# Decoder step with four linear-recurrent mixers: block transposes in the delta-rule inverse, plain copies at score levels 32 and 64, selections over all rows

## The chip, the core and the metric

One core of a Trainium2 chip runs the kernel: TensorE (PE, with its weight loads shown as PEld), VectorE (DVE), ScalarE (ACT), GpSimd (POOL) and SyncE (SP, which issues the DMAs here) work side by side from queues of their own and meet at semaphores. The metric is the time of one execution on the device in microseconds; lower is better.

## What is computed

Two trunk layers over 256 prompt tokens and 8 x 4 sample tokens (288 columns in all), width 1024, f32. Each layer is a half-step SwiGLU network, the token mixing, and a second half-step SwiGLU network, each closed by a layer norm with shift, scale and gate from a conditioning vector. The token mixing has four mixers of four heads: retention, GLA, HGRN2 and gated DeltaNet. Three of them are gated recurrences:

```python
S_t = diag(exp(g_t)) S_{t-1} + k_t v_t^T,  o_t = S_t^T q_t      # _gla_scan
att = einsum('bhtd,bhsd,bhtsd->bhts', qc, kc, decay); o = att @ vc + (qc * exp(G)) @ S
```

The fourth, gated DeltaNet, solves a unit lower triangular system per chunk:

```python
a = where(strict, bc * (kc @ kc.T) * L, 0.0)
tm = eye + a
u = triangular_solve(tm, bc * vc); w = triangular_solve(tm, bc * exp(G) * kc)
delta = u - w @ S
```

## The kernel before

All work is recorded first as operations and then put in order by a scheduler in the file itself (class `Rec`, `schedule`): each operation has a cost and a priority (the longest path behind it), and `LB` adds a shift to the priority by the name of the section (`inv0` is the inverse of layer 0) and the engine. `STAY` lets PE stay with one shape of matmul, `PEN` weighs a change of ScalarE's function table, `HOLD` lets an engine wait for a better operation. Almost every operation therefore has the helper's line, L547, in the profile, and is found by its tiles.

The large products (feed-forward, the input projections of the mixing `win`, its output projection `wout`) are made of three matmuls each: ScalarE rounds a weight tile to `whi`, VectorE subtracts it to `wlo`, and PE multiplies `whi` with the high and low halves of the input (`hh`, `hl`) and `wlo` with `hh`. Weights come by DMAs of 512 KB on SP's queue into three buffers `st`. The conditioning weights (`ada_w`) come on the same queue into four buffers `ast` and are multiplied in between (`psum_ada`). SP's queue is in order: a load whose buffer is still in use holds all that is behind it.

The mixing (`mixers`) runs, as far as the scheduler lets it: the front of DeltaNet, of GLA and HGRN2 (projections), the inverse, the gates, DeltaNet's middle and back substitution, the scores of HGRN2 (tiles with A, `psum_phA`) and GLA (tiles with B, `psum_phB`), then retention.

`gdn_inverse` builds the inverse X of 16 blocks of 64 by doubling, with levels m = 1, 2, 4, 8, 16, 32 and a last step that joins two blocks to 128. The blocks lie 8 side by side (`q`) in two halves of the rows (`e`), so that a level is 16 small matmuls of 64x64 each, `py`, a ScalarE copy of it into `Y`, and 32 more, `px`: one half gives the new part of X, the other the new part of its transpose XT, each written by a predicated copy under a mask (`mk_x`, `mk_xt`). The 32 sample rows have a small inverse of their own beside it (`Xs`, `XTs`, levels 1 and 2).

`gla_core` builds the scores D of HGRN2 and GLA by levels too: `diag(m, half, mask, smask)` multiplies keys with the half of the queries of this level into one PSUM tile and copies it into D under a mask on VectorE; between levels VectorE multiplies the decay of the level into keys and queries (`tot`).

`gdn_front` spreads rows of the gate tile R (4 heads, at rows 0 to 3 or 64 to 67) over 128 rows by a matmul with a constant of 4 rows (`selp`, `selh`).

Of the kernel before, what the change touches and what calls it, by code (L numbers as in the profile page):

```python
# [12 lines left out]
AF = mybir.ActivationFunctionType  # L13
# [7 lines left out]
LOOK, STAY = 40, 20  # L21
SWITCH = 0.19
PEN, PACE = 8, 1.5
HOLD, HFRAC = {'DVE': 20, 'ACT': 20}, 0.6
LB = {'hg1': 12, 'retf0': -29, 'gdnf1': 15, 'glf0': 30, 'wout1': -6, 'gla1': 5, 'hgf1': 8, 'gdnb1': 19, 'norm11': -2, ('ret1', 'DVE'): 10, 'norm00': -20, ('norm02', 'DVE'): -20, ('ffn12', 'DVE'): -23, 'ret1': 4, 'glf1': -10, 'hgf0': -15, 'ffn11': -26, ('inv0', 'ACT'): -45, 'norm02': -15, ('norm12', 'DVE'): 2, ('norm11', 'ACT'): 2, ('ret0', 'DVE'): 15, 'ffn12': 22, ('norm00', 'DVE'): 6, 'norm12': 88, ('inv1', 'PE'): 8, 'ffn01': 7, 'gdnb0': -6, ('retf1', 'ACT'): 12, ('ffn02', 'DVE'): -2, ('norm00', 'PE'): 12, 'retf1': -8, ('gdnf1', 'DVE'): 4, ('ffn01', 'ACT'): -15, ('wout1', 'DVE'): -30, 'hg0': -30, ('gates1', 'DVE'): 6, ('gdnf1', 'PE'): -15, ('inv0', 'DVE'): -4, 'norm10': -31, ('gdnb0', 'DVE'): 30, 'inv0': -11, ('norm10', 'PE'): 2, 'wout0': 15, ('hgf0', 'ACT'): -30, ('gla0', 'PE'): 2, ('hgf1', 'PE'): -4, 'gdnf0': -2, ('gates1', 'ACT'): -15, ('norm12', 'ACT'): 30, ('gla1', 'ACT'): -15, ('retf0', 'ACT'): 8, 'gates0': -8, ('glf0', 'ACT'): 30, ('norm02', 'ACT'): -4, ('norm00', 'ACT'): -4, ('gates0', 'DVE'): 2, ('wout1', 'ACT'): -30, ('gdnf1', 'ACT'): -2, 'gates1': 4}
WIN, WARM, WARMUP = 3.413, 0.3, 20.0
KEEP, KEEP2 = 0, 0.05
# [110 lines left out]
class Rec:  # L138
# [168 lines left out]
    def schedule(self):  # L307
# [54 lines left out]
        while len(order) < len(ops):  # L362
# [27 lines left out]
            elif e == "PE":  # L390
# [11 lines left out]
                if dense:  # L402
                    j = next((k for k, x in enumerate(top) if ops[x[1]].act > 0.5 * ops[x[1]].cost), 0)
                else:
                    j = next((k for k, x in enumerate(top) if ops[x[1]].tiled == tiled and x[0] < top[0][0] + STAY), 0)
# [709 lines left out]
class Mixer:  # L1115
# [62 lines left out]
    def gdn_front(self, l, h):  # L1178
# [144 lines left out]
    def gdn_inverse(self):  # L1323
# [16 lines left out]
        G_.tensor_copy(Xs[SP], bc(idn, 1, 4))  # L1340
# [5 lines left out]
        f8 = lambda t: t.rearrange("p h c t -> p (h c) t")  # L1346
        X8, XT8, Y8, NA8 = f8(X), f8(XT), f8(Y), f8(NA)
# [7 lines left out]
        for li, m in enumerate(INV_LEVELS[:-1]):  # L1355
            cols = lambda t: t.rearrange("p h (n m) -> p h n m", m=m)
            py = self.pst([P, 8, 32], "ps")
            if m == 1:
                for e in range(2):
                    V.copy_predicated(qhalf(XT8[R[e]], 1, 1), mk8(self.mk_xt(0)[R[e]], 1), qhalf(NA8[R[e], :, 64 * e:64 * e + 64], 1, 1))  # L1360
                for q, r, pos, cc in each8():
                    self.mm(py[r, q, :], NA8[r, q, cc], halves(self.ident[r, cc], 1)[0], pos=pos)
                V.copy_predicated(qhalf(X8, 1, 0), mk8(self.mk_x(0), 1), cols(py))
            else:
                for q, r, pos, cc in each8():
# [731 lines left out]
```

## Time and profile before

| | us |
|---|---|
| three runs, median (lowest to highest) | 1525.8 (1521.66 to 1527.0) |
| the profiled execution | 1528.0 |
| its span, first to last instruction | 1526.2 |
| PE busy in it | 1450.7 |
| DVE busy | 922.0 |
| ACT busy | 710.4 |
| POOL busy | 112.9 |

The mean granted clock of TensorE is 0.962. The mixing of layer 0 lies at about 260 to 560 us, that of layer 1 at about 1010 to 1290 us; the rest is feed-forward and norms. An idle engine costs nothing as long as PE is full; a stretch with PE busy may still be slow, where the granted clock is low.

### The profile page before, as it was taken

How to read it: one execution, taken by the hardware profiler on the slowest of the kernel's cores; microseconds unless marked ns; L12 is line 12 of the kernel's file. 1: busy time of each engine (PE TensorE's matmuls, PEld its weight loads, DVE VectorE, ACT ScalarE, POOL GpSimd, SP SyncE). 2: the span in 40 equal slices, each digit the busy share in tenths (PEclk: the TensorE clock that was granted, in tenths of full speed). 3: DMA queues.
4: the chain of work that ended last, by engine and by line, in shares of the span. 5: the costliest groups of instructions: out<-in, count | busy, mean ns of one | idle time of the engine just before them, and what ended most of it. 6: DMA issues, size and time to landing. Idle time of an engine off the chain costs nothing.

```text
span 1526.2 us, 32521 instructions
## 1 busy us (share of the span) xinstructions
PE 1450.7 (95%) x13172; PEld 1355.8 (89%) x13172; DVE 922.0 (60%) x2076; ACT 710.4 (47%) x1447; POOL 112.9 (7%) x193
## 2 busy tenths in 40 slices
PE   7999999899999979999999999989999998999996
PEld 6899998798887769999999999977989776999996
DVE  3755556776445786555675555567674868755564
ACT  4744434753303456444465444457523325644443
POOL 0000002200003210000000000012001231000000
PEclk9999999899959989999999999999999998999998
DMA  9955675745714645555565556547322254555530
GB/s 365 353 176 165 210 274 199 262 148 197 256 65 160 219 173 182 168 165 166 165 214 187 167 165 209 167 147 249 114 84 66 80 196 161 179 167 166 169 123 32
DMA packets 80215, 271.11 MB, mean 178 GB/s; under 512 B 9376, under 2 KB 12992, under 8 KB 80064
## 3 DMA queue, kind: packets, MB, share of 16 engines
q1 hardware_dynamic: 80064, 269.03, 52.6%
q8 instruction: 103, 1.69, 0.4%
q14 instruction: 48, 0.39, 0.1%
HBM read 263.52 MB, written 5.47 MB: 176 GB/s over the span
## 4 chain that ended last, share of the span: by engine, by line
PE 81%; DVE 9%; DMA 4%; ACT 4%; issue 1%; SPq 0%; ACTq 0%; DVEq 0%; POOL 0%
PE psum_acc L547 47%; PE psum_ps L547 24%; DVE base_d L547 3%; PE psum_ada L547 3%; PE psum_phA L547 3%; PE psum_phB L547 3%; DMA base_st<-win 2%; PE psum_oa L547 1%; ACT base_tmp L547 1%; DMA base_ast<-ada_w 1%; DVE base_wlo L547 1%; ACT base_whi L547 1%; DVE base_hl L547 1%; DVE base_tmp L547 1%; DVE base_xa L547 1%
## 5 line engine op out<-in xcount | busy, mean ns | idle before, releaser
L547 ACT ACTIVATE base_whi<-base_st 128x512 fp32r<-128x512 f32 x410 | 252.3, 624 | 264.4 <-PE psum_acc L547 186.3
L547 DVE TENSOR_TENSOR base_wlo<-base_st,base_whi 128x512 fp32r<-128x512 f32 x410 | 282.9, 698 | 143.4 <-ACT base_whi L547 133.2
L547 DVE TENSOR_TENSOR gp_wlog<-gp_stg,gp_whig 128x512 fp32r<-128x512 f32 x274 | 188.0, 690 | 262.3 <-ACT gp_whig L547 241.9
L547 ACT ACTIVATE gp_whig<-gp_stg 128x512 fp32r<-128x512 f32 x274 | 171.6, 629 | 284.0 <-PE psum_acc L547 254.6
L547 PE MATMUL psum_ps<-base_hh,base_whi 128*128 128x288 f32 x760 | 197.6, 301 | 8.2 <-ACT base_hh L547 7.9
L547 PE MATMUL psum_ps<-base_hl,base_whi 128*128 128x288 f32 x760 | 191.1, 298 | 0.0
L547 PE MATMUL psum_ps<-base_hh,base_wlo 128*128 128x288 f32 x760 | 189.8, 298 | 0.5 <-DVE base_wlo L547 0.5
L547 PE MATMUL psum_acc<-base_hh,gp_whig 128*128 128x288 f32 x648 | 169.5, 303 | 5.1 <-ACT base_hh L547 4.9
L547 PE MATMUL psum_acc<-base_hh,base_whi 128*128 128x288 f32 x552 | 159.5, 321 | 10.0 <-ACT base_hh L547 3.9
L547 PE MATMUL psum_acc<-base_hl,gp_whig 128*128 128x288 f32 x648 | 164.7, 296 | 0.0
L547 PE MATMUL psum_acc<-base_hh,gp_wlog 128*128 128x288 f32 x648 | 158.7, 295 | 0.0
L547 PE MATMUL psum_acc<-base_hl,base_whi 128*128 128x288 f32 x552 | 156.0, 312 | 0.7 <-DVE base_hl L547 0.6
L547 PE MATMUL psum_acc<-base_hh,base_wlo 128*128 128x288 f32 x552 | 153.4, 310 | 0.8 <-DVE base_wlo L547 0.8
L547 PEld LDWEIGHTS psum_ps<-base_hh,base_whi 128*128 128x128 f32 x760 | 134.6, 191 | 14.4 <-ACT base_hh L547 9.0
L547 PEld LDWEIGHTS psum_ps<-base_hl,base_whi 128*128 128x128 f32 x760 | 133.3, 191 | 0.5 <-DVE base_hl L547 0.4
L547 PEld LDWEIGHTS psum_ps<-base_hh,base_wlo 128*128 128x128 f32 x760 | 132.7, 191 | 0.8 <-DVE base_wlo L547 0.8
L547 PEld LDWEIGHTS psum_acc<-base_hh,gp_whig 128*128 128x128 f32 x648 | 113.1, 189 | 9.5 <-ACT base_hh L547 6.8
L547 PEld LDWEIGHTS psum_acc<-base_hh,base_whi 128*128 128x128 f32 x552 | 103.9, 200 | 19.1 <-ACT base_hh L547 5.6
L547 PE MATMUL psum_acc<-gp_gh,gp_whig 128*128 128x288 f32 x384 | 113.7, 296 | 0.0
L547 PEld LDWEIGHTS psum_acc<-base_hl,gp_whig 128*128 128x128 f32 x648 | 113.1, 189 | 0.5 <-DVE base_hl L547 0.4
L547 PE MATMUL psum_acc<-gp_gl,gp_whig 128*128 128x288 f32 x384 | 113.4, 295 | 0.0
L547 PE MATMUL psum_acc<-gp_gh,gp_wlog 128*128 128x288 f32 x384 | 113.4, 295 | 0.0
(425 smaller groups left out, 2699.3 us busy)
## 6 DMA issues: line engine op xcount, KB each, us to landing
base_ast<-ada_w SPq DMA_DIRECT2D x135, 512.0 KB, 6.4
gp_stg<-wi SPq DMA_DIRECT2D x82, 512.0 KB, 3.9
base_st<-wi SPq DMA_DIRECT2D x82, 512.0 KB, 3.6
base_st<-win SPq DMA_DIRECT2D x60, 512.0 KB, 3.6
gp_stg<-wo SPq DMA_DIRECT2D x48, 512.0 KB, 3.6
base_st<-wo SPq DMA_DIRECT2D x40, 512.0 KB, 4.0
base_st<-wout SPq DMA_DIRECT2D x16, 512.0 KB, 4.3
gp_stg<-wi SPq DMA_DIRECT2D x14, 256.0 KB, 6.6
```

Of the source, the lines that this page charges most:

```text
L547: getattr(getattr(nc, o.fn[0]), o.fn[1])(*[conv(a) for a in o.args], **{k: conv(v) for k, v in o.kw.items()})
```

## The change

The inverse. At level 1, XT is set from the input under its mask as before, and X is its 32x32 block transpose on VectorE. At levels 2 to 16 `px` has 16 matmuls instead of 32, for X alone, and XT is again a block transpose of the whole X. At level 32 the new block of X is moved by a ScalarE copy, and the block of XT is a transpose from 32 rows to the 32 rows above. `Y` is filled in one piece, so that its clearing goes, and the start values of X go. The sample rows get the transpose at level 1.

The scores. At levels 32 and 64 of `diag` ScalarE copies the blocks that are wanted, two or one, with no mask.

The selections take all 128 rows of R against constants with zeros in the other rows (`sel`, broadcast along its columns, and `selp`).

The scheduler. New numbers in its table `LB` and its constants, and a new rule by which PE waits a little for a matmul of the shape it is in.

```diff
-LOOK, STAY = 40, 20
+LOOK, STAY, STAY2 = 40, 30, 50
+PWAIT, PHOLD = 0.2, 20
-PEN, PACE = 8, 1.5
-HOLD, HFRAC = {'DVE': 20, 'ACT': 20}, 0.6
-LB = {'hg1': 12, 'retf0': -29, 'gdnf1': 15, 'glf0': 30, ...
+PEN, PACE = 5, 1
+HOLD, HFRAC = {'DVE': 1000000000.0, 'ACT': 40}, 0.6
+LB = {'hg1': 12, 'retf0': -29, 'gdnf1': 11, 'glf0': 16, ...
-KEEP, KEEP2 = 0, 0.05
+KEEP, KEEP2 = 0, 0
...
+            if e == "PE" and ops[i].tiled != tiled and fut[e]:
+                a, j = fut[e][0]
+                if a < t + PWAIT and ops[j].tiled == tiled and ops[j].prio > ops[i].prio - PHOLD:
+                    heapq.heappush(avail[e], (-ops[i].prio, i))
+                    free[e] = a
+                    dense, run = save
+                    continue
...
-            self.mm(pe, self.selp[0:4, p, :], R[0:4, :])
+            self.mm(pe, self.selp[:, p, :], R)
...
-        G_.memset(g["Y"], 0.0)
...
-            self.mm(pg, self.selh[q4, hd, :], R[q4, :], pos=(64, 0))
+            self.mm(pg, self.sel[:, hd:hd + 1].to_broadcast([P, P]), R)
...
-            V.tensor_copy(flat(X[R[e]]), bc(idb, 1, 8))
...
-                for q, r, pos, cc in each8():
-                    self.mm(py[r, q, :], NA8[r, q, cc], halves(self.ident[r, cc], 1)[0], pos=pos)
-                V.copy_predicated(qhalf(X8, 1, 0), mk8(self.mk_x(0), 1), cols(py))
+                V.transpose(row(X8), row(XT8))
...
-                A.activation(qhalf(Y8, m, 0), cols(py), AF.Copy)
-                px = self.pst([P, 2, 8, 32], "ps")
+                A.activation(Y8[:, :, 0:32], py, AF.Copy)
+                px = self.pst([P, 8, 32], "ps")
                 for q, r, pos, cc in each8():
-                    self.mm(px[r, 0, q, :], XT8[r, q, :], halves(Y8[r, q, :], m)[0], pos=pos)
-                    self.mm(px[r, 1, q, :], Y8[r, q, :], halves(XT8[r, q, :], m)[1], pos=pos)
-                V.copy_predicated(qhalf(X8, m, 0), mk8(self.mk_x(li), m), cols(px[:, 0]))
-                V.copy_predicated(qhalf(XT8, m, 1), mk8(self.mk_xt(li), m), cols(px[:, 1]))
+                    self.mm(px[r, q, :], XT8[r, q, :], Y8[r, q, 0:32], pos=pos)
+                if m < 32:
+                    V.copy_predicated(qhalf(X8, m, 0), mk8(self.mk_x(li), m), cols(px))
+                    V.transpose(row(XT8), row(X8))
+                else:
+                    for e in range(2):
+                        up, lo = slice(64 * e, 64 * e + 32), slice(64 * e + 32, 64 * e + 64)
+                        A.activation(X8[lo, :, 0:32], px[lo], AF.Copy)
+                        V.transpose(XT8[up, :, 32:64], X8[lo, :, 0:32])
...
+            if m >= 32:
+                for b in range(P // (2 * m)):
+                    kb = slice(2 * m * b, 2 * m * b + m)
+                    A.activation(D[kb, :, 2 * m * b + m:2 * m * b + 2 * m], ps.rearrange("p c h t -> p (c h) t")[kb, :, m * b:m * b + m], AF.Copy)
+                return
```

What the new order looks like is shown at three places of layer 0. The first is PE in the inverse. `psum_ps<-base_d` are its matmuls, `psum_phA<-mx_qxA,mx_kA` the scores of HGRN2, `psum_ada` the conditioning, `psum_acc<-base_hh,...` a projection. Before, one level (m = 16) reads:

```order
L547 MATMUL psum_ps_62<-base_d_79 64x32 x16
L547 MATMUL psum_phA_64<-mx_qxA_2750,mx_kA_2749 32x32 x2
L547 MATMUL psum_ada_66<-base_ast_108,base_cs_76 32x128 x4
L547 MATMUL psum_acc_60<-base_hh_82,base_wlo_104 128x288
L547 MATMUL psum_ps_63<-base_d_79 64x32 x32
L547 MATMUL psum_phA_64<-mx_qxA_2750,mx_kA_2749 128x128 x4
```

Now the last level (m = 32) and the start of the join read:

```order
L555 MATMUL psum_ps_63<-base_d_79 64x32 x16
L555 MATMUL psum_phA_64<-mx_qxA_2750,mx_kA_2749 128x128 x4
L555 MATMUL psum_ps_62<-base_d_79 64x32 x16
L555 MATMUL psum_phA_64<-mx_qxA_2750,mx_kA_2749 128x256 x2
L555 MATMUL psum_ps_63<-base_d_79 64x64 x8
```

The block of 32 is one of 16, a level of scores stands between any two blocks, and the projections that stood there have moved behind the back substitution.

The second is VectorE at the same place, from the predicated copy of a level of scores (`mx_DA`) on. Before, at the end of the inverse:

```order
L547 COPY_PREDICATED mx_DA_2769<-base_mku_113,psum_phA_64 128x64x8
L547 COPY_PREDICATED base_d_79<-base_mku_113,psum_ps_63 128x8x32 x2
L547 TENSOR_TENSOR mx_qxA_2750<-mx_qxA_2750,mx_tot16A_2774 128x2x8x16
L547 TENSOR_TENSOR mx_kA_2749<-mx_kA_2749,mx_tot16A_2774 128x8x16
L547 TENSOR_TENSOR mx_qxA_2750<-mx_qxA_2750,mx_tot16A_2774 128x2x8x16
```

Now, from level 16 of the inverse on:

```order
L555 COPY_PREDICATED mx_DA_2769<-base_mku_113,psum_phA_64 128x32x16
L555 COPY_PREDICATED base_d_79<-base_mku_113,psum_ps_63 128x16x16
L555 STREAM_TRANSPOSE base_d_79<-base_d_79 128x512
L555 TENSOR_TENSOR mx_qxA_2750<-mx_qxA_2750,mx_tot32A_2775 128x2x4x32 x2
L555 TENSOR_TENSOR mx_kA_2749<-mx_kA_2749,mx_tot32A_2775 128x4x32 x2
L555 TENSOR_TENSOR mx_qxA_2750<-mx_qxA_2750,mx_tot64A_2776 128x2x2x64 x2
L555 TENSOR_TENSOR mx_kA_2749<-mx_kA_2749,mx_tot64A_2776 128x2x64 x2
L555 STREAM_TRANSPOSE base_d_79<-base_d_79 32x8x32 x2
```

One predicated copy and a transpose stand where two predicated copies stood, and the two last levels of scores have no copy on VectorE.

The third is SP's queue at the end of the mixing: the last two loads of projection weights (`win`) and the state outputs around them. Before:

```order
L547 DMA base_ast_105<-ada_w 128x1024
L547 DMA base_ast_106<-ada_w 128x1024
L547 DMA out_hgrn_p<-mx_SoA_2779 128x128
L547 DMA base_st_85<-win 128x1024
L547 DMA base_ast_107<-ada_w 128x1024
L547 DMA out_gla_p<-mx_SoB_2791 128x64
L547 DMA base_st_87<-win 128x1024
L547 DMA out_gdn_s<-base_d_79 128x1024
```

Now:

```order
L555 DMA base_ast_105<-ada_w 128x1024
L555 DMA base_ast_106<-ada_w 128x1024
L555 DMA base_st_85<-win 128x1024
L555 DMA out_gdn_p<-mx_Sog_2759 128x128
L555 DMA base_st_87<-win 128x1024
L555 DMA base_st_85<-wout 128x1024
```

The two loads of `win` stand ahead of the outputs of HGRN2 and GLA; the run of `ada_w` loads in front of them, not shown in full, is 12 long where it was 15.

## Rows read from the trace of the kernel before

**Rows 1.** The page, first part: engines, busy us, share of the span, instructions.

```profile
PE 1450.7 (95%) x13172; PEld 1355.8 (89%) x13172; DVE 922.0 (60%) x2076; ACT 710.4 (47%) x1447; POOL 112.9 (7%) x193
```

**Rows 2.** Stretches of 20 us: busy us, instructions by engine, granted clock, DMA share, GB/s.

```profile
core 0: us, PE busy (x) PEld busy (x) DVE busy (x) ACT busy (x) POOL busy (x), PEclk, DMA share, GB/s
...
100.00:120.00 20.00, 20.00 (x152) 19.95 (x151) 9.22 (x16) 8.18 (x16) 0.00 (x0) 1.00 0.54 164
...
420.00:440.00 20.00, 19.74 (x270) 17.27 (x271) 8.85 (x21) 1.15 (x3) 0.00 (x0) 0.50 0.15 43
440.00:460.00 20.00, 20.00 (x237) 18.15 (x238) 9.09 (x24) 0.59 (x1) 0.61 (x1) 0.73 0.27 85
...
1020.00:1040.00 20.00, 17.84 (x160) 14.86 (x159) 15.04 (x38) 17.38 (x37) 1.85 (x13) 0.98 0.45 160
...
1180.00:1200.00 20.00, 18.08 (x231) 14.28 (x232) 17.97 (x34) 2.72 (x7) 5.25 (x5) 1.00 0.15 49
```

**Rows 3.** The same view, three stretches of layer 0's mixing.

```profile
408.00:452.00 44.00, 40.48 (x588) 35.74 (x589) 17.66 (x43) 6.12 (x14) 0.61 (x1) 0.57 0.29 101
452.00:476.00 24.00, 23.98 (x361) 20.12 (x354) 13.05 (x36) 3.98 (x9) 4.02 (x4) 1.00 0.41 137
476.00:506.00 30.00, 26.15 (x303) 17.86 (x303) 17.72 (x40) 13.89 (x31) 14.82 (x16) 0.89 0.65 223
```

**Rows 4.** Groups by form, layer 0's mixing: busy us, mean ns, idle before.

```profile
L547 PE MATMUL psum_ps<-base_d 64*64 64x32 f32 x480 | 24.6, 273 | 3.3 <-DVE base_d L547 2.0 <-ACT mx_gYs L547 1.3
...
L547 PE MATMUL psum_ps<-base_tmp,base_cf 128*128 128x288 f32 x8 | 3.9, 577 | 1.4 <-DVE mx_gEs L547 0.8 <-ACT base_tmp L547 0.6
L547 PE MATMUL psum_ps<-mx_gR,base_cf 4*128 4x288 f32 x12 | 3.7, 427 | 0.0
...
L547 PE MATMUL psum_ps<-base_ident,base_d 64*64 64x32 f32 x32 | 1.1, 220 | 0.0
```

**Rows 5.** The same, layer 1's mixing.

```profile
L547 PE MATMUL psum_ps<-base_d 64*64 64x32 f32 x480 | 16.7, 225 | 0.0
```

**Rows 6.** Instructions in order of time, layer 0's inverse: start, us.

```profile
399.50 0.42 PE L547 MATMUL psum_ps<-base_ident,mx_gEs 32*32 32x16 f32 x8
...
427.05 1.65 PE L547 MATMUL psum_phA<-mx_qxA,mx_kA 128*128 128x128 f32 x6
427.17 0.76 DVE L547 COPY_PREDICATED base_d<-base_mku,psum_ps 128x256 f32<-128x256 uint8 x2 [4.46 <-PE psum_ps L547]
...
430.65 0.38 ACT L547 ACTIVATE base_d<-psum_ps 128x256 f32<-128x256 f32 x1 [8.22 <-PE psum_ps L547]
...
431.79 3.63 PE L547 MATMUL psum_ps<-base_d 64*64 64x32 f32 x64
...
437.03 0.42 DVE L547 TENSOR_TENSOR mx_qxA<-mx_qxA,mx_tot4A 128x256 f32<-128x256 f32 x1 [0.80 <-PE psum_phA L547]
...
437.38 0.28 DVE L547 TENSOR_TENSOR mx_kA<-mx_kA,mx_tot4A 128x128 f32<-128x128 f32 x1
...
438.12 0.70 DVE L547 COPY_PREDICATED mx_DA<-base_mku,psum_phA 128x512 f32<-128x512 uint8 x1
```

**Rows 7.** Groups by form, whole program, ACT and DVE.

```profile
L546 ACT ACT_TABLE_LOAD x28 | 35.9, 1283 | 1.2 <-PEq L2084 0.7
...
L547 ACT ACTIVATE base_d<-psum_ps 64x512 f32<-64x512 f32 x2 | 1.2, 592 | 17.6 <-PE psum_ps L547 17.6
...
L547 DVE COPY_PREDICATED mx_DA<-base_mku,psum_phA 128x512 f32<-128x512 uint8 x16 | 15.0, 937 | 4.7 <-PE psum_phA L547 4.7
...
L547 DVE TENSOR_SCALAR mx_S0A<-mx_S0A,base_cf 128x512 f32<-128x512 f32 x4 | 1.9, 482 | 0.1
```

**Rows 8.** SP's DMA issues in order of time, end of layer 0's mixing.

```profile
492.56 0.42 SPq L547 DMA_DIRECT2D out_hgrn_p<-mx_SoA  x1
493.25 0.33 SPq L547 DMA_DIRECT2D base_st<-win  x1
...
498.28 0.33 SPq L547 DMA_DIRECT2D base_st<-win  x1
```

More of the change, by code (lines that the diff above doesn't have):

```diff
@@ L404, in schedule @@
                 else:
-                    j = next((k for k, x in enumerate(top) if ops[x[1]].tiled == tiled and x[0] < top[0][0] + STAY), 0)
+                    j = next((k for k, x in enumerate(top) if ops[x[1]].tiled == tiled and x[0] < top[0][0] + (STAY if tiled == (128, 128) else STAY2)), 0)
                 i = top[j][1]
@@ L1346, in gdn_inverse @@
         f8 = lambda t: t.rearrange("p h c t -> p (h c) t")
+        row = lambda t: t.rearrange("p q t -> p (q t)")
         X8, XT8, Y8, NA8 = f8(X), f8(XT), f8(Y), f8(NA)
@@ L1356, in gdn_inverse @@
             cols = lambda t: t.rearrange("p h (n m) -> p h n m", m=m)
-            py = self.pst([P, 8, 32], "ps")
             if m == 1:
@@ L1360, in gdn_inverse @@
                     V.copy_predicated(qhalf(XT8[R[e]], 1, 1), mk8(self.mk_xt(0)[R[e]], 1), qhalf(NA8[R[e], :, 64 * e:64 * e + 64], 1, 1))
-                for q, r, pos, cc in each8():
-                    self.mm(py[r, q, :], NA8[r, q, cc], halves(self.ident[r, cc], 1)[0], pos=pos)
-                V.copy_predicated(qhalf(X8, 1, 0), mk8(self.mk_x(0), 1), cols(py))
+                V.transpose(row(X8), row(XT8))
             else:
+                py = self.pst([P, 8, 32], "ps")
                 for q, r, pos, cc in each8():
@@ L1374, in gdn_inverse @@
             if m <= 2:
                 X_, XT_, NA_, Y_ = Xs[SP], XTs[SP], NAs[SP], Ys[SP]
-                py = self.pst([P, 4, 16], "ps")
                 if m == 1:
                     V.copy_predicated(qhalf(XT_, 1, 1), mk(self.mk_sxt(0)[SP], 1), qhalf(NA_, 1, 1))
-                    for hd in range(4):
-                        self.mm(py[SP, hd, :], NA_[:, hd, :], halves(idn, 1)[0], pos=(96, 96))
-                    V.copy_predicated(qhalf(X_, 1, 0), mk(self.mk_sx()[SP], 1), cols(py[SP]))
+                    V.transpose(X_.rearrange("p h t -> p (h t)"), XT_.rearrange("p h t -> p (h t)"))
@@ L1382, in gdn_inverse @@
                 else:
+                    py = self.pst([P, 4, 16], "ps")
                     for hd in range(4):
@@ L1858, in mix_setup @@
         self.blk = cf["blk"]
-        self.selh = cf["selh"].rearrange("p (h m) -> p h m", h=4)
-        self.selp = cf["selh"][:, 0:256].rearrange("p (h m) -> p h m", h=2)
+        self.sel = cf["sel"]
+        self.selp = cf["selp"].rearrange("p (h m) -> p h m", h=2)
         self.reset = cf["reset"]
@@ L1905 @@
 CF, CFN = {}, 0
-for _n, _c in (("caus", 128), ("scaus", 32), ("bmask", 8), ("blk", 128), ("selh", 512), ("reset", 288), ("rgam", 4)):
+for _n, _c in (("caus", 128), ("scaus", 32), ("bmask", 8), ("blk", 128), ("sel", 4), ("selp", 256), ("reset", 288), ("rgam", 4)):
     CF[_n] = (CFN, _c)
@@ L1954, in consts @@
     put("blk", (i[:, None] // 64) == (i[None] // 64))
-    selh = np.zeros((4, 4, P))
-    selp = np.zeros((4, 2, P))
+    sel, selp = np.zeros((P, 4)), np.zeros((P, 2, P))
     for h in range(4):
-        selh[h, h] = 1
+        sel[64 + h, h] = 1
         selp[h, h // 2, 64 * (h % 2):64 * (h % 2) + 64] = 1
-    put("selh", selh.reshape(4, 512), slice(64, 68))
-    o[0:4, CF["selh"][0]:CF["selh"][0] + 256] = selp.reshape(4, 256)
+    put("sel", sel)
+    put("selp", selp.reshape(P, 256))
     c = np.arange(NT)
```

3 lines of the change are left out of this document (1 added, 2 removed).

## The prediction

> **What bounds the kernel now.** I read the page's engine lines first: TensorE (PE) is busy for 1450.7 us of a span of 1526.2 us, and no other engine comes near it [rows 1]. So time goes away only where PE work goes away, where PE stops waiting, or where PE's clock rises. The second view is the row of 20 us windows. In a feed-forward stretch (100 to 120 us) PE is busy 20.00 of 20 us at granted clock 1.00, and nothing can be won there. In the mixing of layer 0 the window 420 to 440 us has PE busy for 19.74 us but at clock 0.50, which is the lower of its two levels (1.2 GHz), and the next window has 0.73 [rows 2]. The third view cuts the same place by what runs there: from 408 to 452 us, the inverse with the scores of one mixer beside it, the mean clock is 0.57 and PE stands still for 44.00 - 40.48 = 3.5 us; from 452 to 476 us, the back substitution, the clock is 1.00 again; from 476 to 506 us PE stands still for 3.85 us at 0.89 [rows 3]. The fourth view, PE's instructions by form, says how much of this the change touches: the inverse's 64x64 matmuls with 32 columns take 24.6 us in layer 0 and 16.7 us in layer 1 [rows 4, 5]. An f32 matmul makes two records, so 480 records are 240 matmuls.
>
> **The change part by part.** My sum is made against the profiled execution, 1528.0 us.
>
> *Inverse, matmuls.* Each of five levels now has 16 + 32 matmuls, and the second 32 build both X and its transpose. The change builds X alone and gets the transpose by a VectorE block transpose, so 16 of 48 go: a third of 480 records. The first level loses its 16 matmuls with the identity and 4 small ones of the sample rows. Layer 0: 24.6 / 3 = 8.2, + 1.1 [rows 4], + 0.4 for the small ones [rows 6], 9.7 us. At half clock throughout, with 1.8 us for 32 records (half of the 3.63 us for 64, [rows 6]), it would be 5 x 1.8 + 1.5 = 10.5; at layer 1's prices it would be 7.1. Layer 1: 16.7 / 3 = 5.6 [rows 5], + the same 1.1 + 0.4 = 7.1 us. Nothing covers this work: PE is full around it. **-9.7 and -7.1.**
>
> *Inverse, VectorE and ScalarE.* Four levels per layer had two predicated copies (0.76 us the pair, [rows 6]) and have one and a 128x512 transpose; the first level's transpose replaces a predicated copy and a copy of the identity. The trace has no VectorE transpose. Its nearest rows are 128x512 forms: 0.48 us the cheapest, 0.94 the mean predicated copy [rows 7]; I take 0.70, the predicated copy at contiguous levels [rows 6]. So VectorE has about 0.3 us more per level. The transpose is needed by the second matmuls of the next level only, behind 16 matmuls and the ScalarE copy (1.8 + 0.38 us, [rows 6]), so it hides, unless VectorE is late with the scores' work. That is the give-back: in layer 0 each block of 16 now stands with one level of scores beside it instead of 48 matmuls and more, and a level of scores keeps VectorE for 2 x 0.42 + 2 x 0.28 us of products and 0.70 us of copy [rows 6], 2.1 us, 2.6 with its half of the inverse's, and an estimated 3.9 to 4.5 us with the scores' own matmuls (1.65 us, [rows 6]) ahead of them. PE's own half level at half clock is 1.8 + 1.65 us and two switches of shape, some 4.0 us. The two are level, so PE waits 0 to 0.5 us in 8 half levels: **+2** (0 to +4). VectorE: DVE Perf Modes, The three transpose paths, of the Trainium skill gives 311 ns for a 128x128 bf16 transpose; four of these, 1.24 us, would be an estimate for 128x512 by that page, and the sum 2 us later; no run here shows it yet.
>
> *Levels 32 and 64.* Per scores two predicated copies go from VectorE (8 in all x 0.70 = 5.6 us) and three ScalarE copies come (8 of 32 partitions, bounded by 0.38 [rows 6], and 4 of 64x512 at 0.59 [rows 7], some 5.4 us). ScalarE is busy 47% of the span, so it covers this; without that cover it costs 5.4. VectorE's relief is felt where PE waits for it: in 1180 to 1200 us VectorE is busy 17.97 us and PE idle 1.92 [rows 2]. **-1** (0 to -1.9).
>
> *Selections.* 12 records per layer change from 4 to 128 rows with the same 288 columns; a 4-row one has 427 ns, a 128-row one 577, but that mean comes from single ones with a wait before them [rows 4]. **0** (-0.8 for fewer switches of shape to +3.6).
>
> *Order.* The table of shifts and the scheduler's constants are new, so everything around moves. I hold to two places. In layer 0 the two last weight loads of the mixing now stand ahead of the state outputs on SP's queue and behind three fewer loads of the conditioning weights. Before, the first of them was issued at 493.25 us, right behind an output at 492.56, the second at 498.28 [rows 8], and PE had little to do: 3.85 us idle and 0.11 x 30 = 3.3 us lost to the clock [rows 3]. **-3** (0 to -7.1). And ScalarE has four more table loads at 1.28 us [rows 7], all in the heads of the mixing, where ScalarE is busy 17.38 of 20 us [rows 2]: **+1.5** (0 to +5.1).
>
> **Sum:** -9.7 - 7.1 + 2 - 1 - 3 + 1.5 = -17.3, so 1510.7 against 1528.0. The median of the runs, 1525.8, is 2.2 under the profiled execution; for a median I say **1509**. With each term at its better end it is 1499, with each at its worse end no gain.
>
> **The rivals.**
>
> *The clock stays low for longer* (no measurable change). In layer 0 the rows from level m = 4 of the inverse to the end of the back substitution hold no projection at all now, where before projections stood between. The back substitution ran at 1.00 for 24 us with PE busy 23.98 [rows 3]. If half of that falls to 0.50, it takes some 12 us longer: 1509 + 12 = 1521. For it: the inverse itself ran at 0.50 with PE never idle. Against it: the share of full-array matmuls per inverse matmul rises.
>
> *The clock stays up* (faster still). PE's 3.5 us of waiting ahead of the inverse [rows 3] came with the fall of the clock. If the new order loses that wait and the stretch runs at 1.00, the 8 half levels are held by VectorE at some 3.9 us each, 31 us, where the forecast leaves 44 - 9.7 + 2 = 36; with the 3.5 us of waiting 8.5 us more go: 1500. TensorE: Matmul & The Clock Gate, Why this matters for your kernels, of the Trainium skill, says that a TensorE kept busy without gaps is given the full clock, and by that rule this rival would be the forecast. The trace does not bear it out: 19.74 us busy of 20 stood at 0.50 [rows 2].
>
> *Slower.* The same clock, further: the back substitution of layer 0 all at half clock (+24 from [rows 3]) and layer 1's inverse, which ran mostly warm, at layer 0's prices (24.6 - 16.7, two thirds of it left, +5). That is 1509 + 29 = 1538. It decides from 24.4 us of loss on (1533.4), or some 49 us more at half clock than before. Against it: in layer 1 projections stand between all blocks.
>
> *The change does not do what it says:* the row of built instructions shows 160 + 32 + 8 fewer matmuls over both layers, so this is out.
>
> **How the numbers follow.** Forecast (1503 to 1517) 0.55; clock up 0.14; clock low for longer 0.22; slower 0.09. What a measurement here tells from no change is about 0.5%, 7.6 us. Faster by more than that (under 1518.2) has the forecast and the clock up, and a little of the third: 0.72. Same 0.19, slower 0.09. The range leaves out the slow rival and the far ends: 1496 to 1525.
>
> **What would show it.** Right: 320 records of the 64x32 form per layer with the same price each; transposes near 0.7 us on VectorE, PE not waiting for them; the stretch of the inverse in layer 0 some 9 us shorter; no stand of PE for the last weights of layer 0. Wrong: transposes of several us; a clock of 0.50 behind the inverse; PE waiting for VectorE's products between half levels; new waits for weights, since all projections of retention in layer 0 now stand behind the inverse.

## The result and the profile after

The changed kernel takes 1483.5 us (median of 4 runs, 1481.3 to 1486.7) against 1525.9 before: a ratio of 0.974 with a 95% interval of 0.9711 to 0.977. It is faster, as forecast, but by 42 us where 17 were forecast, and below the range of 1496 to 1525. Its profiled execution took 1486.7 us.

The page of the kernel after begins with its span and the engines (busy us, share of the span, instructions); it answers to [rows 1].

```profile
span 1484.9 us, 31728 instructions
PE 1408.8 (95%) x12772; PEld 1324.1 (89%) x12772; DVE 912.1 (61%) x2064; ACT 717.6 (48%) x1467; POOL 115.0 (8%) x189
```

TensorE's (PE's) busy time fell by 41.9 us, and the span less its busy time stayed (75.5 before, 76.1 now). So the whole gain lies inside PE's busy time. It is more than the work that went away, and the next view says why: the same stretches as in [rows 2, 3], of the kernel after (us, then busy us and instructions of PE, PEld, DVE, ACT, POOL, then the granted clock, DMA share, GB/s).

```profile
420.00:440.00 20.00, 18.25 (x315) 16.34 (x313) 13.38 (x37) 4.05 (x9) 0.61 (x1) 1.00 0.43 154
440.00:460.00 20.00, 17.35 (x273) 15.47 (x271) 9.13 (x22) 5.39 (x13) 7.13 (x8) 1.00 0.57 193
...
408.00:452.00 44.00, 39.94 (x805) 35.67 (x803) 27.45 (x69) 8.68 (x20) 6.74 (x8) 1.00 0.53 183
452.00:476.00 24.00, 19.80 (x176) 15.88 (x176) 15.62 (x29) 12.57 (x27) 9.26 (x10) 0.93 0.51 166
476.00:506.00 30.00, 30.00 (x276) 24.29 (x273) 23.77 (x62) 12.78 (x26) 6.71 (x6) 1.00 0.60 196
```

Where the clock was 0.50 with PE busy for 19.74 of 20 us, it is 1.00 with PE busy for 18.25. PE idles more and does more: 805 instructions in the 44 us that held 588. Over the whole program the mean granted clock rose from 0.962 to 0.987 (over all runs on record, 0.962 to 0.976 before and 0.986 to 0.987 now). At levels of 0.5 and 1 that is (1 - 0.962) x 2 x 1526.2 = 116 us at the low clock before and 39 now; the trace's clock records, without the end behind the last matmul, give 106 and 31. What that cost can be counted record by record: what a PE instruction adds to the busy time at the low clock, less the mean of its form at the full clock in the same trace. It comes to 46.7 us before and 14.1 now, 32.6 less, of which 20.8 lie in the stretch of layer 0's mixing and 4.9 in that of layer 1's.

The instructions that the edits bring cost what was forecast. Groups by form of the kernel after, first of layer 0's mixing (layer 1's row of the 64x32 form reads the same), then of the whole program (busy us, mean ns, idle before).

```profile
L555 PE MATMUL psum_ps<-base_d 64*64 64x32 f32 x320 | 11.9, 220 | 0.0
...
L555 PE MATMUL psum_ps<-mx_gR,base_cf 128*128 128x288 f32 x12 | 3.9, 432 | 0.6 <-DVE base_d L555 0.6
...
L555 DVE STREAM_TRANSPOSE base_d<-base_d 128x512 f32<-128x512 f32 x10 | 7.1, 710 | 0.3
...
L555 ACT ACTIVATE mx_DA<-psum_phA 32x256 f32<-32x256 f32 x4 | 1.5, 371 | 4.1 <-PE psum_phA L555 4.1
...
L555 ACT ACTIVATE mx_DA<-psum_phA 64x512 f32<-64x512 f32 x2 | 1.2, 592 | 1.6 <-PE psum_phA L555 1.6
...
L554 ACT ACT_TABLE_LOAD x32 | 41.1, 1283 | 1.3 <-PEq L2097 0.7
```

By place, from the first output column of one network to that of the next (the rows whose right operand is `base_ones`), the stretch with layer 0's mixing is 355.0 us before and 331.4 now, that with layer 1's 316.8 and 301.9; the other five together lose 2.8 us.

### The profile page after: what moved, and what is told of

It reads as the page before. It is cut to its first block, busy times and chain, and to the rows that moved or that the text cites. A ratio compares the mean times of both kernels' runs of the same rounds, so it can differ in the third digit from the quotient of the medians.

```text
span 1484.9 us, 31728 instructions
## 1 busy us (share of the span) xinstructions
PE 1408.8 (95%) x12772; PEld 1324.1 (89%) x12772; DVE 912.1 (61%) x2064; ACT 717.6 (48%) x1467; POOL 115.0 (8%) x189
## 4 chain that ended last, share of the span: by engine, by line
PE 79%; DVE 10%; ACT 5%; DMA 3%; issue 2%; POOL 0%; SPq 0%; DVEq 0%; ACTq 0%; POOLq 0%
PE psum_acc L555 47%; PE psum_ps L555 23%; DVE base_d L555 3%; PE psum_phB L555 3%; PE psum_ada L555 3%; PE psum_phA L555 3%; ACT base_whi L555 1%; DVE base_wlo L555 1%; DVE base_tmp L555 1%; PE psum_oa L555 1%; ACT base_tmp L555 1%; ACT L554 1%; DMA base_ast<-ada_w 1%; DMA base_st<-win 1%; DVE base_hl L555 1%
## 5 line engine op out<-in xcount | busy, mean ns | idle before, releaser
L555 PE MATMUL psum_ps<-base_hh,base_whi 128*128 128x288 f32 x760 | 191.2, 298 | 0.8 <-DVE base_rt L555 0.6
L555 PE MATMUL psum_ps<-base_hl,base_whi 128*128 128x288 f32 x760 | 186.7, 298 | 0.0
L555 PE MATMUL psum_ps<-base_hh,base_wlo 128*128 128x288 f32 x760 | 186.1, 297 | 0.0
L555 PE MATMUL psum_acc<-base_hh,base_whi 128*128 128x288 f32 x552 | 153.6, 318 | 15.2 <-ACT base_hh L555 7.2
L555 PE MATMUL psum_acc<-base_hl,base_whi 128*128 128x288 f32 x552 | 149.7, 308 | 0.7 <-DVE base_hl L555 0.7
L555 PE MATMUL psum_acc<-base_hh,base_wlo 128*128 128x288 f32 x552 | 148.4, 307 | 0.0
L555 PEld LDWEIGHTS psum_ps<-base_hl,base_whi 128*128 128x128 f32 x760 | 130.1, 189 | 0.7 <-DVE mx_rto L555 0.2
L555 PEld LDWEIGHTS psum_acc<-base_hh,base_whi 128*128 128x128 f32 x552 | 100.3, 195 | 25.5 <-ACT base_hh L555 8.6
```

The source lines that it names most:

```text
L555: getattr(getattr(nc, o.fn[0]), o.fn[1])(*[conv(a) for a in o.args], **{k: conv(v) for k, v in o.kw.items()})
```

## The experiments

The kernel after differs from before in its work (the inverse, the score levels, the selections) and in its order. To part them, most kernels below freeze an order: the kernel records the work of one version, lets the scheduler order it, records the other work, and gives each operation that both have its old rank; a new one stands right behind its predecessor in the record. Such an order was not made for the work that it gets, and that alone can cost something. Medians are given with the kernel before on the same chip in the same runs, and the ratio with its interval.

### Work and order apart

```diff
-net.nc.emit(tc, net.nc.schedule())
+settings(SCHED, *ORDER_OF); old = Kernel(tc.nc, ia, oa); old.build(); order = old.nc.schedule()
+settings(SCHED, *ALG); net = Kernel(tc.nc, ia, oa); net.build()
+net.nc.emit(tc, net.nc.replay(old.nc, order))
```

The first has `SCHED = "before"`, the order of the old work, and the new work in it.

> The three changes of the work (inverse, levels 32 and 64, selections) in the kernel before, with every instruction that both kernels share kept in the row of the kernel before on its engine; what is new stands right behind its predecessor. The scheduler has no say. Theory 'work': the fewer small matmuls are what keeps TensorE's clock up in the inverse of layer 0, so the low stretch of 37.5 us shrinks to under 10 us and the time is 1485 to 1495 us. Theory 'order': the clock stays low at the same place (over 25 us of it), only the matmuls go, some 10 + 6 us, and the time is about 1510 us.

The second is the converse, `SCHED = "after"`, the order of the new work, and the old work in it.

> The converse: the work of the kernel before (48 matmuls a level, predicated copies at levels 32 and 64, 4-row selections) in the row of the kernel after, frozen. Theory 'work': the clock falls again in the inverse of layer 0, 20 to 40 us at 0.50, and the time is 1515 to 1525 us. Theory 'order': the clock stays up but for 10 us more at most, the 320 records that come back cost 10 x 1.12 us and the first level 2 x 1.5, so about 1498 us.

The other two let the scheduler order anew: new work with the old numbers, old work with the new numbers.

> The work of the kernel after, but put in order anew by the scheduler's numbers of the kernel before (table of shifts and constants). Theory 'work': 1480 to 1495 us. Theory 'order': 1505 to 1520 us, with some 60 us and more at the low clock in all.

> The work of the kernel before, put in order anew by the scheduler's numbers of the kernel after. Theory 'work': 1515 to 1530 us. Theory 'order': 1495 to 1505 us. If the numbers suit only the work that they go with, it is slower than the kernel before, and the difference is spread over the mixing of both layers.

| work, order | median (before) | ratio (interval) | PE busy | span - busy | mean clock |
|---|---|---|---|---|---|
| old, old (before) | | | 1450.7 | 75.5 | 0.962 |
| new, old | 1520.8 (1524.7) | 0.9983 (0.9961 to 1.0005) | 1436.2 | 82.1 | 0.968 |
| old, new | 1515.6 (1524.7) | 0.9937 (0.9911 to 0.9963) | 1432.0 | 78.8 | 0.979 |
| new, new (after) | 1483.5 (1525.9) | 0.974 (0.9711 to 0.977) | 1408.8 | 76.1 | 0.987 |
| new, old numbers | 1510.4 (1524.7) | 0.9893 (0.9832 to 0.9955) | 1436.1 | 72.0 | 0.968 |
| old, new numbers | 1517.3 (1524.7) | 0.9952 (0.9928 to 0.9976) | 1440.2 | 80.2 | 0.970 |

Neither theory holds for all four: 1515.6 and 1517.3 us lie in the ranges of 'work', 1510.4 in that of 'order', 1520.8 in neither. The new work alone gives 0.2%, within its interval of nothing, the new order alone 0.6%, and both together 2.6%. The pages of the two mixed kernels show what each lacks (the line of their spans and clocks, and PE's; first new work in the old order, then old work in the new).

```profile
core 0: 1518.3 us, clock 0.968
PE 1436.2 (95%) x12772; PEld 1343.6 (88%) x12772; DVE 919.8 (61%) x2064; ACT 717.1 (47%) x1463; POOL 110.6 (7%) x189
```

```profile
core 0: 1510.8 us, clock 0.979
PE 1432.0 (95%) x13172; PEld 1342.9 (89%) x13172; DVE 917.5 (61%) x2076; ACT 710.8 (47%) x1451; POOL 115.9 (8%) x193
```

Kernels with the same work issue the same 12772 (or 13172) PE instructions, so where their busy time differs, it is the speed of the same matmuls. The new work runs 27.4 us longer on PE in the old order than in the new, and PE stands 6.0 us more: that is the 33.4 us between their spans. By the count record by record the low clock costs 37.9 us there and 14.1 in the kernel after, so 23.8 of the 33.4, seven tenths, are clock. The other 3.6 of busy time are not clock: in the old order some of the inverse's blocks of 32 records take 1.84 us at the full clock where those of the kernel after take 1.12 (4.4 us in all; other forms are a little faster). And the new work did save matmuls in the old order too (busy 14.5 us less than before), but 6.6 us came back as standing: in layer 0 the inverse's small matmuls alone wait 4.9 us for VectorE, where they waited 2.0 [rows 4].

### Which of the three edits

```diff
-ALG = (True, True, True)    # inverse, levels 32 and 64, selections
+ALG = (False, True, True)   # new_order_old_inverse
+ALG = (True, False, False)  # new_order_inverse_alone
```

> The kernel after with its order frozen, and only the inverse put back (48 matmuls a level, two predicated copies, the first level by matmuls with the identity); levels 32 and 64 and the selections stay as in after. Theory 'the inverse is the change': nearly all of what the old work cost in this order comes back, 1505 to 1516 us: 14 us of matmuls, the rest waits and low clock. Theory 'spread over the three edits': 1495 to 1500 us.

> The converse: the order of after frozen, the inverse as in after, but predicated copies at levels 32 and 64 and the 4-row selections of the kernel before. Theory 'the inverse is the change': 1483 to 1488 us. Theory 'spread': 1490 to 1497 us, since eight copies of 0.7 to 1.0 us stand again in a stretch where TensorE waits for VectorE.

With the old inverse 1510.0 us (before: 1523.3), 0.9902 (0.9872 to 0.9933); with the new inverse alone 1488.7, 0.9768 (0.9737 to 0.9799). The first theory holds, 0.7 us over its range in the second run: the inverse is the change. The other two edits are worth some 5 us at most; the interval of the second run overlaps that of the kernel after.

### What brings the clock down

Four kernels with a frozen order and one kind of dose each.

```diff
-                    V.transpose(row(XT8), row(X8))
+                    for _ in range(4):                       # transposes_x4, both layers
+                        V.transpose(row(XT8), row(X8))
```

> The kernel after, order frozen, with each of the eight 128x512 block transposes of levels 2 to 16 done four times in a row (the result is the same). That is 8 x 3 x 0.71 = 17.0 us more on VectorE. Theory 'TensorE waits for VectorE and that is all': 1493 to 1501 us, the clock in the inverse of layer 0 stays at 1.00 although TensorE idles more. Theory 'waits bring the clock down': a low stretch of over 20 us comes back in the inverse, 1505 us and more. If the transposes are hidden: under 1487 us.

```diff
+                if nc.label == "inv0" and m == 4:            # dose_small
+                    for _ in range(3):
+                        for q, r, pos, cc in each8():
+                            self.mm(py[r, q, :], NA8[r, q, cc], halves(X8[r, q, :], m)[0], pos=pos)
```

> The kernel after, order frozen, with one dose: in layer 0 alone, at level 4, the first 16 matmuls of 64x64 are issued four times (same result), 96 records more, 3 x 1.12 = 3.4 us at the full clock. Theory 'the low clock holds itself' (at half speed the small matmuls fill more of the time, so that it stays low until a run of large ones comes): the clock falls there and stays low for over 20 us, cost 12 to 20 us, 1496 to 1504 us. Theory 'it only follows the moment': at most 7 us at 0.50, cost 3 to 7 us, 1487 to 1491 us.

```diff
                     V.transpose(row(XT8), row(X8))
+                    if nc.label == "inv0" and m == 8:        # one_wait
+                        for _ in range(3):
+                            V.transpose(row(XT8), row(X8))
```

> The kernel after, order frozen, with one block transpose only, that of level 8 in layer 0, done four times (same result): 2.1 us more on VectorE at one place. Theory 'a wait sets the low clock off and the inverse then holds it': TensorE waits some 2.7 us there, the clock falls and stays at 0.50 for 15 us and more with TensorE then hardly waiting; cost 8 to 14 us, 1492 to 1498 us. Theory 'the clock follows the mean load of the stretch': at most 3.4 us low, cost about 2 us, 1485 to 1487 us.

```diff
+                if nc.label == "inv0" and m in (4, 8):       # dose_full, in the kernel before
+                    for hd in range(4):
+                        self.mm(py.rearrange("p q t -> p (q t)"), g["kx"][:, hd, 0:P], g["kx"][:, hd, 0:TP])
```

> The kernel before, order frozen, with two doses of full-size work that nothing needs: four 128x128 matmuls with 256 columns (8 records of some 0.28 us, 2.2 us) ahead of the first 16 matmuls of levels 4 and 8 in layer 0, just behind the two waits (1.30 and 1.98 us) at which the clock fell. They are overwritten. Theory 'a wait among small matmuls sets it off, then it holds itself': the low stretch of 37.5 us shrinks to under 14 us, 12 to 17 us come back less 4.4 us of doses, 1511 to 1518 us: more work, less time. Theory 'the mean load': still over 25 us low, 1526 to 1530 us.

| kernel | median (before) | ratio (interval) | mean clock |
|---|---|---|---|
| transposes_x4 | 1506.9 (1523.3) | 0.9886 (0.9856 to 0.9916) | 0.971 |
| dose_small | 1484.3 (1523.3) | 0.9746 (0.9711 to 0.978) | 0.988 |
| one_wait | 1493.8 (1523.3) | 0.9813 (0.9792 to 0.9834) | 0.974 |
| dose_full | 1515.9 (1523.3) | 0.995 (0.9929 to 0.9971) | 0.979 |

Begin with the place in the kernel before where the clock fell, PE in order of time (start, us, instruction, and in brackets the idle time before it and who ended it):

```profile
408.17 2.17 PE L547 MATMUL psum_ada<-base_ast,base_cs 128*32 128x128 f32 x64
411.63 1.12 PE L547 MATMUL psum_ps<-base_d 64*64 64x32 f32 x32 [1.30 <-ACT mx_gYs L547]
412.69 0.42 PE L547 MATMUL psum_ps<-mx_gXTs,mx_gYs 32*32 32x16 f32 x8
413.04 0.33 PE L547 MATMUL psum_ada<-base_ident,base_adae 128*128 128x128 f32 x1
413.30 3.62 PE L547 MATMUL psum_ps<-base_d 64*64 64x32 f32 x64
```

32 records of the small form take 1.12 us; from 413.30 on 64 take 3.62, which is the low clock. Ahead of it stand 5 us of small forms (matmuls on 64x64, 32x32 and 128x32 tiles) with a wait of 1.30 us among them. Small forms alone need not do it: in `dose_small` 5.9 us of them run without a gap, and the large ones behind still run at full speed (8 records of 128x128 in 1.07 us), the stretch at 1.00. Both ranges on record for this run were missed: it takes 1484.3 us, as the kernel after does, with a dose that fills the wait of 1.53 us that PE has there otherwise.

```profile
406.60 1.95 PE L664 MATMUL psum_ada<-base_ast,base_cs 128*32 128x128 f32 x64
408.49 3.92 PE L664 MATMUL psum_ps<-base_d 64*64 64x32 f32 x128
...
412.51 1.07 PE L664 MATMUL psum_phA<-mx_qxA,mx_kA 128*128 128x128 f32 x8
...
406.00:440.00 34.00, 31.91 (x684) 29.03 (x682) 22.75 (x57) 6.19 (x14) 1.65 (x2) 1.00 0.56 187
```

But they can be followed by the fall as well. In the new work in the old order (`alg_old_order`) PE has no wait over 0.13 us from 407.99 us on, and the clock fell at 414.06, where one large matmul takes 0.61 us instead of 0.40:

```profile
408.34 1.96 PE L657 MATMUL psum_ada<-base_ast,base_cs 128*32 128x128 f32 x64
410.42 1.12 PE L657 MATMUL psum_ps<-base_d 64*64 64x32 f32 x32
411.48 0.42 PE L657 MATMUL psum_ps<-mx_gXTs,mx_gYs 32*32 32x16 f32 x8
411.82 0.33 PE L657 MATMUL psum_ada<-base_ident,base_adae 128*128 128x128 f32 x1
412.08 1.84 PE L657 MATMUL psum_ps<-base_d 64*64 64x32 f32 x32
...
414.10 0.61 PE L657 MATMUL psum_acc<-base_hh,base_whi 128*128 128x288 f32 x1
```

An added wait was followed by it in both runs that have one. `one_wait`, from the block before the added transposes on, and PE's 20 us behind the wait in a row:

```profile
428.68 1.12 PE L664 MATMUL psum_ps<-base_d 64*64 64x32 f32 x32
432.55 2.08 PE L664 MATMUL psum_phA<-mx_qxA,mx_kA 128*128 128x128 f32 x8 [2.76 <-DVE mx_DA L664]
434.56 1.92 PE L664 MATMUL psum_ps<-base_d 64*64 64x32 f32 x32
436.41 2.07 PE L664 MATMUL psum_phA<-mx_qxA,mx_kA 128*128 128x128 f32 x8
...
452.38 1.16 PE L664 MATMUL psum_ps<-mx_qg,mx_kx 128*128 128x128 f32 x8
...
432.00:452.00 20.00, 19.45 (x196) 17.45 (x200) 7.59 (x20) 3.67 (x8) 0.61 (x1) 0.51 0.04 5
```

After one wait of 2.76 us the blocks take 1.92 and 2.07 us instead of 1.12 and 1.16, and PE doesn't wait once for the next 20 us: at half speed VectorE is ready first there. The same rows of the kernel after, from the score block behind level 8 (424.67) to the first `mx_qg,mx_kx` row (436.48), take 11.8 us; here, from 432.55 to 452.38, 19.8. That is 8.0 us behind a wait that is 2.2 us longer, together the 10 us of the medians. So a low clock, once there, held through the rest of the inverse with PE all but full. `transposes_x4` shows the same fall at the same level (a wait of 2.75 us, then 20.5 us low) and costs 23 us in all, six more than its transposes last. (In this profile of `one_wait` some 7 us ahead of the dose, from 417 us, are low as well, which the kernel after doesn't have.)

A shorter wait doesn't settle it. The kernel after still waits 1.53 us at the head of this inverse, behind the same small forms, and stays at 1.00. In `filled_norms_2` (below), with the same matmuls in the same order there, the clock fell for 10.2 us. First the kernel after, then `filled_norms_2`:

```profile
410.09 1.12 PE L555 MATMUL psum_ps<-base_d 64*64 64x32 f32 x32
412.75 0.33 PE L555 MATMUL psum_ada<-base_ident,base_adae 128*128 128x128 f32 x1 [1.53 <-DVE base_adae L555]
412.91 1.08 PE L555 MATMUL psum_phA<-mx_qxA,mx_kA 128*128 128x128 f32 x8
```

```profile
413.01 0.48 PE L664 MATMUL psum_ada<-base_ident,base_adae 128*128 128x128 f32 x1 [2.01 <-DVE base_adae L664]
413.27 1.92 PE L664 MATMUL psum_phA<-mx_qxA,mx_kA 128*128 128x128 f32 x8
```

Six profiles have these matmuls and this wait. The clock fell in two, `filled_norms_2` (2.01 us) and `one_wait` (1.53), and not in the kernel after (1.53), `transposes_x4` (1.53), `filled_norms_4` (1.53) and `new_order_inverse_alone` (2.19). What decides between them is open; with such a wait, a clean inverse is in part luck.

The other way round, with spare matmuls of the full size behind the wait the fall was short. `dose_full`, the kernel before with 16 records more:

```profile
412.41 0.42 PE L664 MATMUL psum_ps<-mx_gXTs,mx_gYs 32*32 32x16 f32 x8 [1.31 <-ACT mx_gYs L664]
...
413.49 3.35 PE L664 MATMUL psum_ps<-mx_kx 128*128 128x256 f32 x8
...
418.38 2.06 PE L664 MATMUL psum_ps<-base_d 64*64 64x32 f32 x64 [0.48 <-ACT base_d L664]
...
413.00:447.00 34.00, 32.72 (x576) 28.69 (x577) 19.02 (x48) 3.28 (x7) 0.61 (x1) 0.95 0.44 155
```

The same wait (1.31 us, and 0.40 behind it) and the same small forms, but 64 records now take 2.06 us, the low stretch is 3.4 us instead of 37.5, and the kernel is 7.5 us faster although it does 5.2 us more. So an added wait of 2.75 us among these matmuls brings a fall that then holds, and full-size matmuls in its place keep it short. A wait is not needed for a fall (`alg_old_order`), a shorter one need not bring it (the kernel after), and why it holds is not shown.

### How particular the order is

```diff
-SWITCH = 0.19
+SWITCH = 0.2          # renumbered_1
-PEN, PACE = 5, 1
+PEN, PACE = 6, 1      # renumbered_2
```

> The kernel after with one number of the scheduler's model changed in its last digit (the price of a change of matmul shape, 0.19 to 0.20 us), put in order anew: the same work, the same table, another order from the second layer norm on. Theory 'the numbers hold a lucky order': 1492 to 1510 us, by a low stretch of over 15 us somewhere or by more idling. Theory 'the numbers make the gain on their own': within 5 us of after.

> The same test by another number: the penalty for a change of ScalarE's table 6 instead of 5. The same two expectations: 1492 to 1510 us, or within 5 us of after.

1508.8 us (before: 1523.3), 0.9916 (0.9897 to 0.9935), and 1510.7, 0.9906 (0.9875 to 0.9938), the second over the seven shorter of ten runs that spread from 1495.5 to 1519.8 (1512.2 over all ten). The work and the table are those of the kernel after, and 25 us and more are gone. PE's busy time is 1426.0 and 1430.0 us at a mean clock of 0.972 and 0.966, its idle time 80.3 and 73.7: the clock again. It is not the same fall each time. `renumbered_2` has one low stretch of 27.3 us in layer 0's inverse; `renumbered_1` has none over 6.8 us, but 75 us low in all against 31. With the old numbers the new work came to 1510.4, with a low stretch of 34.1 us in layer 1's inverse. So three orders that the scheduler makes of the new work by other numbers lie at 1509 to 1511 us.

### What was still open

The new work in the old order once more, with the two doses of `dose_full`:

> The new work in the order of the kernel before (as in the run that gave 1520.75 us), with the same two doses of full-size matmuls that nothing needs, ahead of levels 4 and 8 in layer 0. Theory 'the low clock hid the work's gain': its low stretch of 27.3 us in the inverse shrinks to under 7 us and 5 to 12 us come back, 1508 to 1515 us. Theory 'waits for VectorE hid it': the clock comes up but the time stays, 1519 to 1525 us.

1520.1 us (before: 1523.3), 0.997 (0.9951 to 0.999). That is in the range of the second theory, but no answer, since the doses worked in part only: the low stretch went from 27.3 to 17.1 us, because the clock fell again at 432 us, behind waits of 1.13 and 0.52 us between blocks that are now shorter. What the old order hides is therefore read from PE's busy and idle time above.

And spare matmuls where the kernel after still runs low, in PE's wait behind the sums of the layer norms:

```diff
+        if nc.label in ("norm01", "norm11"):     # filled_norms_4: "norm00", "norm10" with 8 as well
+            spare = self.pst([P, P], "ps")
+            for _ in range(12):
+                self.mm(spare, self.ident, self.ident)
```

> The kernel after, order frozen, with twelve spare 128x128 matmuls (some 3.3 us) behind the sums of the second layer norm of each layer, where TensorE waits 4.1 us for ScalarE's first result and then starts the feed-forward at 0.50 for 6.8 us (layer 0) and 3.4 us (layer 1). Theory 'a wait sets the low clock off, here as in the inverse': both stretches go, 3 to 5 us less, 1478 to 1481 us. Theory 'this low clock has another cause': no change or up to 2 us more.

> As the run before, and eight spare matmuls (2.2 us) behind the sums of the first layer norm of each layer too, where TensorE waits 2.5 and 2.7 us and low stretches of 3.4 and 10.2 us follow in the heads of the mixing. Theory 'waits': 6 to 11 us less than the kernel after, 1473 to 1478 us. Theory 'another cause': 1483 to 1490 us, since the spare matmuls there stand ahead of conditioning matmuls that fill part of the wait already.

1488.1 us, 0.9761 (0.9735 to 0.9788), and 1486.6, 0.9755 (0.9726 to 0.9785). The first output column of the feed-forward behind norm 1 in layer 0, first in the kernel after, then with the wait filled, and the latter's clock:

```profile
542.02 0.61 PE L555 MATMUL psum_acc<-base_hh,gp_whig 128*128 128x288 f32 x1 [4.13 <-ACT base_hh L555]
```

```profile
537.20 2.84 PE L664 MATMUL psum_ps<-base_ident 128*128 128x128 f32 x24
541.49 0.40 PE L664 MATMUL psum_acc<-base_hh,gp_whig 128*128 128x288 f32 x1 [1.46 <-ACT base_hh L664]
...
core 0: 1483.6 us, clock 0.990
```

The first matmul behind the wait now takes 0.40 us instead of 0.61, and the mean clock of the second kernel is the highest of all, 0.990, with 20 us low instead of 31. So in layer 0 filling the wait keeps the clock up there too. In layer 1 it didn't: a low stretch of 3.4 us stands behind the same wait with and without the spare matmuls (from 1254.6 us in the kernel after, from 1253.9 here). And the time is not better than that of the kernel after: in the head of a norm PE waits for ScalarE's and VectorE's next column anyway (0.28 us just behind), and a faster matmul only waits sooner; that this is why is argued. 'Waits' was wrong on both times; of the other theory's ranges 1486.6 us lies in the one and 1488.1 some 3 us over the other. The profile of `filled_norms_2` also has the 10.2 us of low clock shown above. None of the kernels beats the kernel after.

## Why the prediction was wrong on the size

*What went right.* The matmuls: 320 records per layer as forecast, in layer 1 at nearly the price forecast (11.9 us in either layer; for layer 0 see below). In layer 1, where the clock was up before too, 16.7 - 11.9 = 4.8 and 1.5 for the first level and the sample rows, 6.3 us against 7.1 forecast. The transpose costs 710 ns, where 0.70 us was taken from the predicated copy. The estimate from the Trainium skill's page VectorE: DVE Perf Modes, The three transpose paths, would have been 1.24 us; the measurement decides. ScalarE's new copies take 0.37 us (8) and 0.59 us (4), 5.4 us in all, as forecast. The 128-row selections take 432 ns where the 4-row ones took 427: zero, as forecast. PE waits for VectorE between half levels, as the give-back said: 0.34 us once and 0.58 to 0.59 three times, 2.1 us against 2 forecast. But the kernel before waited for VectorE in this place too (1.98 and 0.23 us). From the second sample-row matmuls (`mx_gXs,mx_gEs`, at 407.8 us in both) to the last 64x64 one of the join PE stands 3.5 us before and 3.6 now, so nothing was given back on balance. VectorE and PE side by side in the kernel after, levels 8 and 16 of the inverse in layer 0:

```profile
421.13 0.68 DVE L555 COPY_PREDICATED mx_DA<-base_mku,psum_phA 128x512 f32<-128x512 uint8 x1
421.73 0.42 DVE L555 COPY_PREDICATED base_d<-base_mku,psum_ps 128x256 f32<-128x256 uint8 x1
421.87 1.16 PE L555 MATMUL psum_phA<-mx_qxA,mx_kA 128*128 128x128 f32 x8 [0.58 <-DVE mx_DA L555]
422.18 0.71 DVE L555 STREAM_TRANSPOSE base_d<-base_d 128x512 f32<-128x512 f32 x1
422.84 0.76 DVE L555 TENSOR_TENSOR mx_qxA<-mx_qxA,mx_tot8A 128x256 f32<-128x256 f32 x2
422.96 1.12 PE L555 MATMUL psum_ps<-base_d 64*64 64x32 f32 x32
...
424.67 1.16 PE L555 MATMUL psum_phA<-mx_qxA,mx_kA 128*128 128x128 f32 x8 [0.59 <-DVE mx_DA L555]
```

*The step that failed.* The sum took the clock of the trace before for a property of the work: the inverse of layer 0 was priced at half clock ("PE's own half level at half clock is 1.8 + 1.65"), and no term but the one for SP's order let the clock rise. It goes with the order as well: the new work is low for 27.3 us in layer 0's inverse in the old order and not at all there in the new. The rows on record hinted at it, since the same inverse took 225 ns a record in layer 1 [rows 5] and 273 in layer 0 [rows 4]. In the sum's terms, the matmuls of layer 0's inverse gave 24.6 - 11.9 + 1.5 = 14.2 us instead of 9.7, as the mean record fell from 273 to 220 ns; and all the other matmuls that ran low before had no term. At the full clock the removed work is 2 x (160 x 11.9 / 320 + 1.5) = 14.9 us, near the 16.8 of the sum. The other 27.0 of the 41.9 us of busy time stood in the sum with at most 3.3. They are clock: the count record by record gives 32.6 us less lost to it, and some 5 us go the other way, as the forms that stay take a little longer at the full clock than they did.

*The rival that came nearest was priced too low.* "The clock stays up" (0.14, 1500 us) had the stretch at 1.00. But its condition, that the wait ahead of the inverse goes, did not come true: PE still waits 1.53 us there, and 4.1 us in all from 408 to 452 us where it waited 3.5. That the clock stayed up all the same, no sentence of the prediction foresaw, and by the six profiles above it was not certain. The rival also took a half level to be held by VectorE at 3.9 us, with the scores' matmuls counted ahead of VectorE's work. In the rows above one half level follows the other in 424.67 - 421.87 = 2.80 us, since VectorE's products run beside the inverse's block and only the copy of the scores stands in the way. And it looked at one place. The low time fell in layer 1 as well, from 20.5 to 10.2 us, where its stretch became 14.9 us shorter, against 7.1 of matmuls in the sum.

*The evidence read the wrong way.* That PE was busy for 19.74 of 20 us at 0.50 [rows 2] was held against this rival. Such rows do occur again: `one_wait` has 19.45 of 20 us busy at 0.51, and in `alg_old_order` the clock fell with no wait over 0.13 us in the 6 us ahead. They contradict, as worded, the rule that the prediction cites from the Trainium skill, TensorE: Matmul & The Clock Gate, Why this matters for your kernels, that a TensorE kept busy without gaps is given the full clock. But that a busy PE can stay low doesn't say that it will be low there in the next kernel. That depended on the order around the inverse, and in part on the run.

*The other rivals.* "The clock stays low for longer" and "slower" did not come: the back substitution (441 to 450 us) is at 1.00. The absence of projections between the levels, held to be the danger, did no harm in this order: from 410 to 441 us the clock is 1.00.

*SP's order and the tables.* PE still waits 2.2 us for a last weight of layer 0 at 456.57, so the stand did not go altogether; with the projections moved, its gain can't be told apart, nor can the cost of the four table loads (41.1 us of them in all against 35.9).

*How far the forecast was of the change, and how far of this order.* 1509 us is what the new work gives when the scheduler orders it by numbers one digit off (1509, 1511) or by the old ones (1510). In all three the clock costs somewhat less than before (32.5 to 42.5 us by the count, against 46.7), which the sum did not have, so that they lie at its figure is in part luck. The further 25 us belong to one order, in whose profile the clock stays up through both inverses; over the whole program it is 0.986 to 0.987 in all four runs. The sum had no way to that number, but the range had: 106 us of low clock stood in the trace, and what their loss would give back was not priced beyond one place.

## What to carry to other kernels

Where a stretch stands at the low clock with TensorE full, price the stretch at both clocks, and look at the rows just ahead of it for waits and small matmuls: the state is not a property of the work alone, and it can differ between runs of the same order. Two microseconds of waiting there cost ten here, and a few spare full-size matmuls behind the wait can be cheaper than nothing; where another engine sets the pace, as at the head of a norm, a higher clock bought nothing. When work and order change together, freeze the order to tell them apart, and expect the parts not to add up.

## What the runs showed of the hardware

- The low clock can last: behind one added wait of 2.76 us it was 0.51 for 20 us with PE busy 97% of the time.
- 5.9 us of small matmuls without a gap left the clock at 1.00 (`dose_small`); 6 us of them with no wait over 0.13 us were followed by a fall in `alg_old_order`.
- Waits of 0.58 us behind three blocks of the inverse left it at 1.00. Added waits of 2.75 and 2.76 us among small matmuls were followed by a fall. Waits of 1.53 to 2.19 us behind the same matmuls were followed by one in two profiles of six, and not in the order of their length. One of 1.31 us with full-size matmuls right behind it was followed by 3.4 us of low clock only.
- A block of 32 records of the 64x64 form takes 1.12 us at the full clock and 1.92 at half, not 2.24; some blocks of that form take 1.84 at the full clock (`alg_old_order`, at 412.08 us).
- A block transpose of 128x512 f32 on VectorE takes 710 ns, less than the predicated copy of the scores beside it (1.0 us in the mean).
